# A float32 transformer on one core: the opening reordered, small transfers on GpSimd's queue

## The chip, the cores and the metric

One of the eight cores of a Trainium2 chip runs the kernel. A core has five engines with an instruction stream each: TensorE (PE in the profile, with its weight loads as PEld), VectorE (DVE), ScalarE (ACT), GpSimd (POOL) and SyncE (SP). Each runs its stream in order, and semaphores tie the streams together. Transfers are issued from an engine's queue (SP's, ACT's or POOL's) and are carried out by the core's 16 DMA engines. The metric is the device time of one execution in microseconds (us), the median over several.

## The reference

Input x is [1, 256, 1024], all in float32. Two layers of a block with five branches come first, then a block of gated linear attention with a feed-forward part, modulated by a vector c. Cut to what concerns the opening of the program:

```python
for l in range(2):
    h = rms_norm(x, norm_g[l])
    z = h @ w_in[l]                       # [256, IN_WIDTH], cut into 17 parts
    ...                                   # dsa, mla, diff, sgu branches on parts of z
    kv = rms_norm(mem, mem_norm_g) @ mem_w_kv[l]   # mem is [256, 1024]
    ...                                   # memory branch: attention of a part of z over kv
    x = x + (gates(z) * branches @ w_branch[l]) @ w_out[l]
...                                       # second block: GLA + MoBA, feed-forward 1024 -> 4096 -> 1024,
                                          # both scaled and shifted by silu(c) @ w_ada + b_ada
```

## The kernel before

The products are to have more than half of float32's digits, so each operand is split into a rounded part and a rest: for weights ACT writes `wh` (line 381) and DVE the rest `wl` (line 382), for activations ACT writes `hi` (line 579) and DVE `lo` (line 580). A weight matrix comes in pieces of 512 rows by 512 columns, held as four K tiles of 128 rows ([128, 4, 512], 1 MB). For each piece `mm_tok` runs 12 products for each of the two row tiles of 128 tokens: `wh·hi` and `wl·hi` for the four K tiles in turn (lines 431 and 432), then four `wh·lo` (line 434). 24 such products are a piece.

`run_stream` feeds the pieces through: `load(i)` issues piece i on SP's queue, AHEAD pieces early; `split(i)` makes `wh` and `wl`, LOOK pieces early, into LOOK + 1 = 4 pairs of buffers. Pieces 0 and 1 are two column groups (dv and du, which the sgu branch uses) times the first 512 rows, pieces 2 and 3 the same columns times the other 512 rows; pieces 4 and 5 are aq, 6 and 7 are 452 columns from ak on, and after one piece of `w_ada`, which DVE alone uses (lines 1330 and 1332), come the pieces of `mem_w_kv`. Piece 0 is loaded K tile by K tile.

The x operand is made in halves of 512 columns: `first_x(c)` transposes eight 128x128 blocks on PE (line 576 in `to_operand_g`) and splits them with the gain `norm_g` as a column (`gcol`); `gains_t(0)` has transposed that gain on PE (line 214) into `gT`. `gains_t(1)` does so for the other small vectors, which POOL's queue fetches in `first_loads`. Half 1 of x, `first_x(1)`, stands between pieces 0 and 1.

Work beside the pieces is written as generators in three lanes. `half(k)` is called after each row tile of a piece: it counts down what was deferred with `defer(fn, halves)` and steps lane 0 after the first row tile (k = 0), lanes 1 and 2 after the second. `angles` (rope tables) and behind it `mem_pre` stand in lane 1. `mem_pre` loads the two tiles of mem (line 739), takes four sums of squares on ACT (line 629), adds them up (line 747), makes the reciprocal root on DVE, scales the tiles there (line 750) and transposes them in 16 blocks for `mem_w_kv` (line 576).

A scheduler decides at build time how all this is interleaved: it fixes the order of each engine's stream from dependences and its own estimates, save where `pin` holds instructions at their place. The chip keeps that order. The lines of `evac_scaled` (729) scale and copy a finished sum from PSUM by the row factor `s`.

Of the kernel before, what the change touches and what calls it, by code (L numbers as in the profile page):

```python
# [57 lines left out]
def block_kernel(ctx: ExitStack, tc: tile.TileContext, a, out):  # L58
# [109 lines left out]
    def load_x(c):  # L168
        for t in range(2):
            SY.dma_start(x[t][:, c * 512:c * 512 + 512], xin[tsl(t), c * 512:c * 512 + 512])  # L170
# [5 lines left out]
    SY.dma_start(gains[0][:16, :], as_rows(a["norm_g"], 16))  # L176
    load_x(0)
# [14 lines left out]
    for _ in range(8):  # L192
        T.matmul(warm, ones, ones, start=True, stop=True)
# [48 lines left out]
    def angles():  # L242
        pf = small(8)
# [5 lines left out]
        yield  # L249
# [103 lines left out]
    def run_stream():  # L353
# [3 lines left out]
        def load(i):  # L357
# [3 lines left out]
            if i == 0:  # L361
                for k in range(nk):
                    SY.dma_start(v[:, k, :], bass.AP(tensor=src.tensor, offset=src.offset + k * src.ap[1][0],
                                                     ap=[src.ap[0], src.ap[2]]))
            else:
                SY.dma_start(v, src)
# [23 lines left out]

        load(0)
        load_x(1)
        load(1)
# [12 lines left out]
        pinned.extend(pieces[1:LOOK])  # L406
        for i in range(1, LOOK):
            split(i)
        for i in range(N):
            if i == 1:  # L410
                first_x(1, None)
# [4 lines left out]
            if i + LOOK < N and not late:  # L416
                split(i + LOOK)
# [6 lines left out]
            if i + LOOK < N and late:  # L424
                split(i + LOOK)

    def mm_tok(ps, xo, k0, hi, lo, nk, n, first, last, t):
# [5 lines left out]
        for i in range(nk):  # L433
            T.matmul(ps[:, :n], xo.lo[:, k0 + i, tsl(t)], hi[:, i, :n], start=False,  # L434
                     stop=last and i == nk - 1)

# [65 lines left out]
    def chunk_pair(ap, ops, cols, evacs, pres=None, post=None, rows=(0, 512), by_tile=False):  # L502
# [10 lines left out]
        for j in range(2):  # L513
            for q, (c0, n) in enumerate(cols):
                def fn(hi, lo, j=j, q=q):
                    if j == 0:
                        st[q] = [mbank(), mbank()]
                    if j == 0 or not by_tile:
# [50 lines left out]
    def to_operand_g(srcs, xo, n, g, step=None):  # L569

        for i0 in range(0, n, 2):
# [5 lines left out]
            for i in ks:  # L577
# [4 lines left out]
                if step:  # L582
                    step(i)

# [193 lines left out]
    def layer(l, h):  # L778
# [18 lines left out]
        def sgu():  # L797
            wr = slot([128, 8, 128])
            SY.dma_start(wr, a["sgu_w"][l].rearrange("g i j -> i g j"))
            lng, lnb = work([128, 512], "ln"), work([128, 512], "ln")  # L800
            SY.dma_start(lng, bc_row(a["sgu_ln_g"][l], 512))
            SY.dma_start(lnb, bc_row(a["sgu_ln_b"][l], 512))
# [152 lines left out]
        def diff_prep():  # L955
            lt = work([128, 256], "lam", bufs=1)
            SY.dma_start(lt, bc_row(a["diff_lambda"][l], 256))
            dg = wrk.tile([128, 128], F32, tag="dg", name=nm("dg"), bufs=1)
            SY.dma_start(dg, bc_row(a["diff_norm_g"][l], 128))
# [4 lines left out]
            V.tensor_scalar(dg, dg, 1.0 - LAM[l], None, op0=OP.mult)  # L964
# [810 lines left out]
```

## Time and profile before

| | |
|---|---|
| median of 3 runs | 1231.11 us (1230.07 to 1232.33) |
| the profiled execution | 1232.42 us, of it 1230.5 us span |
| PE busy | 1211.6 us, 98% of the span |
| DVE busy, ACT busy | 903.7 us (73%), 664.5 us (54%) |
| POOL busy | 14.8 us (1%) |
| DMA | 231.30 MB, mean 188 GB/s |

The span runs from the first to the last instruction that the profiler saw; the execution is 1.92 us longer. The granted clock of PE is given as a share of full speed (2.4 GHz), so 0.50 is 1.2 GHz.

### The profile page before, as it was taken

To read this page: it belongs to the slowest core of one execution; us is meant where nothing else is said; L and a number is where in the kernel's file an instruction comes from. 1 tells how busy PE (TensorE), PEld (TensorE's weight loads), DVE (VectorE), ACT (ScalarE), POOL (GpSimd) and SP (SyncE) were. 2 spreads that over 40 slices of the span, in tenths; PEclk is the share of its full clock that TensorE was granted. 3 is DMA by queue.
4 is the path that set the end of the run, shared out by engine and by line. 5 is a ranking of instruction groups with operands and counts; after the bars stand their busy time and mean duration, and the time that the engine had idled before them with its cause. 6 is when DMAs were issued, how large, how long until landed. Compare 5 with 4: busy or idle time off the path is not lost.

```text
span 1230.5 us, 17201 instructions
## 1 busy us (share of the span) xinstructions
PE 1211.6 (98%) x6497; PEld 1044.2 (85%) x6497; DVE 903.7 (73%) x1887; ACT 664.5 (54%) x1161; POOL 14.8 (1%) x35
## 2 busy tenths in 40 slices
PE   9999999999999999999999999999999999999997
PEld 7799888898888888898888988888878877899995
DVE  6866778768896777776887788876685877757665
ACT  6744645567465455546444756555455655545442
POOL 3000000000000000000000000000000000000000
PEclk9999999999999999999999999999988999999999
DMA  8855465544566465755565535656357724757650
GB/s 303 306 181 199 137 206 189 178 153 156 163 220 205 138 206 186 250 172 171 171 211 192 172 124 189 206 172 218 109 171 265 255 85 163 223 188 243 233 174 35
DMA packets 121284, 231.30 MB, mean 188 GB/s; under 512 B 5421, under 2 KB 17009, under 8 KB 121073
## 3 DMA queue, kind: packets, MB, share of 16 engines
q1 hardware_dynamic: 120880, 230.12, 56.8%
q8 instruction: 51, 0.84, 0.3%
q14 instruction: 33, 0.26, 0.1%
q0 software_dynamic: 320, 0.08, 0.1%
HBM read 229.10 MB, written 2.63 MB: 188 GB/s over the span
## 4 chain that ended last, share of the span: by engine, by line
PE 91%; DVE 4%; ACT 1%; DMA 1%; issue 1%; SPq 0%; ACTq 0%
PE pm L431 22%; PE pm L432 22%; PE pm L434 22%; PE pm L446 3%; PE pm L444 3%; PE pm L447 3%; PE po L703 3%; PE pm L552 3%; DVE wl L382 2%; PE pm L683 2%; DMA wt<-in_w_in_dram 1%; PE pm L1100 1%; PE pm L988 1%; PE pm L851 1%; PE po L434 1%
## 5 line engine op out<-in xcount | busy, mean ns | idle before, releaser
L382 DVE TENSOR_TENSOR wl<-wt,wh 128x1024 fp32r<-128x1024 f32 (+3 forms) x386 | 443.3, 1175 | 174.2 <-ACT wh L381 173.6
L381 ACT ACTIVATE wh<-wt 128x1024 fp32r<-128x1024 f32 (+3 forms) x386 | 379.5, 1019 | 272.1 <-PE pm L434 168.0
L431 PE MATMUL pm<-wh,hi 128*128 128x512 f32 (+4 forms) x1320 | 521.0, 396 | 4.0 <-ACT hi L598 2.6
L432 PE MATMUL pm<-wl,hi 128*128 128x512 f32 (+4 forms) x1320 | 509.5, 387 | 0.0
L434 PE MATMUL pm<-wh,lo 128*128 128x512 f32 (+4 forms) x1320 | 348.0, 384 | 0.0
L431 PEld LDWEIGHTS pm<-wh,hi 128*128 128x128 f32 x1320 | 251.3, 190 | 52.6 <-ACT hi L598 4.7
L432 PEld LDWEIGHTS pm<-wl,hi 128*128 128x128 f32 x1320 | 251.3, 190 | 45.6 <-DVE wl L382 0.6
L434 PEld LDWEIGHTS pm<-wh,lo 128*128 128x128 f32 x1320 | 246.5, 189 | 47.5
L446 PE MATMUL pm<-lo,wh 128*128 128x256 f32 x352 | 99.8, 284 | 2.9 <-DVE lo L580 2.9
L444 PE MATMUL pm<-hi,wh 128*128 128x256 f32 x352 | 100.6, 286 | 0.0
L447 PE MATMUL pm<-hi,wl 128*128 128x256 f32 x352 | 99.6, 284 | 0.0
L656 ACT ACTIVATE w<-w,s 128x256 f32<-128x256 f32 (+1 forms) x112 | 49.9, 446 | 39.0 <-DVE s L653 39.0
L446 PEld LDWEIGHTS pm<-lo,wh 128*128 128x128 f32 x352 | 67.8, 193 | 3.6 <-DVE lo L580 3.1
L444 PEld LDWEIGHTS pm<-hi,wh 128*128 128x128 f32 x352 | 67.9, 193 | 0.3
L447 PEld LDWEIGHTS pm<-hi,wl 128*128 128x128 f32 x352 | 67.7, 192 | 0.1
L1332 DVE SCALAR_TENSOR_TENSOR w<-wt,cact,w 128x512 f32<-128x512 f32 x84 | 62.7, 747 | 1.7 <-DMA wt<-in_w_ada_dram 0.6
L1146 ACT ACTIVATE t<-pm,s 128x512 f32<-128x512 f32 x40 | 27.5, 688 | 43.6 <-PE pm L434 43.6
L703 PEld LDWEIGHTS po<-t,w 128*128 128x128 f32 x352 | 46.0, 191 | 2.9
L552 PE MATMUL pm<-ident,t 128*128 128x128 f32 (+1 forms) x332 | 43.8, 273 | 1.6 <-DVE t L1282 1.6
L703 PE MATMUL po<-t,w 128*128 128x64 f32 (+1 forms) x352 | 44.8, 270 | 0.0
L552 PEld LDWEIGHTS pm<-ident,t 128*128 128x128 f32 (+1 forms) x332 | 38.4, 137 | 7.4 <-issue 2.4
L629 ACT ACTIVATE j<-t 128x512 f32<-128x512 f32 (+3 forms) x60 | 28.8, 479 | 28.1 <-DVE t L1682 14.1
(282 smaller groups left out, 1005.1 us busy)
## 6 DMA issues: line engine op xcount, KB each, us to landing
wt<-in_w_in_dram SPq DMA_DIRECT2D x99, 1024.0 KB, 5.0
wt<-in_w_ff_dram SPq DMA_DIRECT2D x32, 1024.0 KB, 5.4
wt<-in_w_ada_dram SPq DMA_DIRECT2D x24, 1024.0 KB, 5.2
wt<-in_w_branch_dram SPq DMA_DIRECT2D x20, 1024.0 KB, 5.1
wt<-in_w_out_dram SPq DMA_DIRECT2D x12, 1024.0 KB, 5.1
wt<-in_mem_w_kv_dram SPq DMA_DIRECT2D x8, 1024.0 KB, 7.3
wt<-in_w_in_dram SPq DMA_DIRECT2D x4, 904.0 KB, 5.5
wt<-in_w_in_dram SPq DMA_DIRECT2D x4, 768.0 KB, 4.4
```

The source lines that it names most:

```text
L381: pin(A.activation(hv[:, ks], wv[:, ks], AF.Copy), on)
L382: pin(V.tensor_tensor(lv[:, ks], wv[:, ks], hv[:, ks].bitcast(F32), OP.subtract), on)
L431: T.matmul(ps[:, :n], xh, hi[:, i, :n], start=first and i == 0, stop=False)
L432: T.matmul(ps[:, :n], xh, lo[:, i, :n], start=False, stop=False)
L434: T.matmul(ps[:, :n], xo.lo[:, k0 + i, tsl(t)], hi[:, i, :n], start=False, stop=last and i == nk - 1)
L444: T.matmul(ps, wh, xh, start=first and i == 0 and c % 2 == 0, stop=False, skip_group_check=True)
L446: T.matmul(ps, wh, xl, start=False, stop=False, skip_group_check=True)
L447: T.matmul(ps, wl, xh, start=False, stop=last and i == nk - 1, skip_group_check=True)
L552: T.transpose(ps[:, i, :], src[:, i * w:(i + 1) * w], ident)
L656: A.activation(p[:, k, :], p[:, k, :], AF.Exp, bias=mx[:, k:k + 1], scale=-1.0, accum_out=sm[:, k:k + 1])
L703: T.matmul(opsum[t][:, h, :], pt[:, k * nb + b, :], u["v"](h, b), start=b == 0, stop=b == nb - 1)
L1332: V.scalar_tensor_tensor(acc, w[:, i, :], B["c"][:, k:k + 1], acc, op0=OP.mult, op1=OP.add)
```

## The change

Of x, half 0 is fetched in four transfers of 256 columns instead of two of 512. `norm_g` and the first two K tiles of piece 0 are issued on ACT's queue, and a small activation behind them makes ACT load its function table there. Piece 1 is issued before half 1 of x. Two more warming products stand behind the first four transposes of x. Piece 0 is computed K tile by K tile for both row tiles (`mm_by_k`). The second half of x is deferred by three halves, so that it stands between the row tiles of piece 1, and the splits ahead are issued by `split_to`. `angles` goes to lane 0, with more steps, which leaves `mem_pre` first in lane 1. Some twenty small transfers (rows of gains and biases, `sgu_w`, the parameters of the second block) go from SP's queue to POOL's. In `diff_attn` one scaling of `dg` is folded into another instruction.

```diff
-    def load_x(c):
-        for t in range(2):
-            SY.dma_start(x[t][:, c * 512:c * 512 + 512], xin[tsl(t), c * 512:c * 512 + 512])
+    def load_x(c, n=512):
+        for c0 in range(c * 512, c * 512 + 512, n):
+            for t in range(2):
+                SY.dma_start(x[t][:, c0:c0 + n], xin[tsl(t), c0:c0 + n])
...
-    SY.dma_start(gains[0][:16, :], as_rows(a["norm_g"], 16))
-    load_x(0)
+    A.dma_start(gains[0][:16, :], as_rows(a["norm_g"], 16))
+    load_x(0, 256)
...
-    for _ in range(8):
-        T.matmul(warm, ones, ones, start=True, stop=True)
+
+    def warming(n):
+        for _ in range(n):
+            pin(T.matmul(warm, ones, ones, start=True, stop=True))
+
+    warming(8)
...
     def angles():
+        yield
...
-        yield
+        for _ in range(3):
+            yield
...
                 for k in range(nk):
-                    SY.dma_start(v[:, k, :], bass.AP(tensor=src.tensor, offset=src.offset + k * src.ap[1][0],
-                                                     ap=[src.ap[0], src.ap[2]]))
+                    q = A if k < 2 else SY
+                    q.dma_start(v[:, k, :], bass.AP(tensor=src.tensor, offset=src.offset + k * src.ap[1][0],
+                                                    ap=[src.ap[0], src.ap[2]]))
+                A.activation(first_act, ones[:, 0:1], AF.Copy)
...
         load(0)
+        load(1)
         load_x(1)
-        load(1)
         first_loads()
...
-        pinned.extend(pieces[1:LOOK])
-        for i in range(1, LOOK):
-            split(i)
+        pinned.extend(pieces[1:LOOK + 1])
+        split(1)
+        ahead = [2]
+
+        def split_to(i):
+            while ahead[0] <= min(i, N - 1):
+                split(ahead[0])
+                ahead[0] += 1
+
+        def second_x():
+            first_x(1, lambda i: None)
+            split_to(LOOK)
+
+        defer(second_x, 3)
         for i in range(N):
-            if i == 1:
-                first_x(1, None)
...
-            if i + LOOK < N and not late:
-                split(i + LOOK)
+            if i > 1 and not late:
+                split_to(i + LOOK)
...
+    def mm_by_k(ps, xo, hi, lo):
+
+        for i in range(4):
+            for t in range(2):
+                xh, xl = xo.hi[:, i, tsl(t)], xo.lo[:, i, tsl(t)]
+                T.matmul(ps[t], xh, hi[:, i, :], start=i == 0, stop=False)
+                T.matmul(ps[t], xl, hi[:, i, :], start=False, stop=False)
+                T.matmul(ps[t], xh, lo[:, i, :], start=False, stop=False)
...
+                    if by_k and j == 0 and q == 0:
+                        mm_by_k(st[q], ops[j](), hi, lo)
+                        half(0)
+                        half(1)
+                        return
...
+            if step and i0 == 0 and xo is E["x"][0]:
+                warming(2)
...
-            SY.dma_start(wr, a["sgu_w"][l].rearrange("g i j -> i g j"))
+            G.dma_start(wr, a["sgu_w"][l].rearrange("g i j -> i g j"))
             lng, lnb = work([128, 512], "ln"), work([128, 512], "ln")
-            SY.dma_start(lng, bc_row(a["sgu_ln_g"][l], 512))
-            SY.dma_start(lnb, bc_row(a["sgu_ln_b"][l], 512))
+            G.dma_start(lng, bc_row(a["sgu_ln_g"][l], 512))
+            G.dma_start(lnb, bc_row(a["sgu_ln_b"][l], 512))
...
-            V.tensor_scalar(dg, dg, 1.0 - LAM[l], None, op0=OP.mult)
...
-                V.tensor_tensor(ov, ov, dg[:, None, :].to_broadcast([128, 4, 128]), OP.mult)
+                V.scalar_tensor_tensor(ov, ov, 1.0 - LAM[l], dg[:, None, :].to_broadcast([128, 4, 128]), op0=OP.mult,
+                                       op1=OP.mult)
...
-            SY.dma_start(B["bias"][p], bass.AP(tensor=d.tensor, offset=d.offset + 384 * p + 127,
+            G.dma_start(B["bias"][p], bass.AP(tensor=d.tensor, offset=d.offset + 384 * p + 127,
...
-    lanes[1].add(angles())
+    lanes[0].add(angles())
     lanes[1].add(mem_pre())
```

Three places of the built programs show what moved. Names end in buffer numbers, which differ between the two programs; line 576 of before is line 609 after, 431 is 450, 432 is 451, 434 is 453, 382 is 391, and 750 is 785.

PE's stream where the blocks of mem (`t_424` and `t_425` before) are transposed; `pm_506` is the second row tile of piece 7. Before:

```order
L431 MATMUL pm_506<-wh_429,hi_133 128x452
L432 MATMUL pm_506<-wl_430,hi_133 128x452
L434 MATMUL pm_506<-wh_429,lo_134 128x452 x4
L576 MATMUL pm_598<-ident,t_424 128x128
L576 MATMUL pm_598<-ident,t_425 128x128
```

After, where `pm_448` is the second row tile of piece 5 and `pm_579` the first product of piece 6 (452 columns):

```order
L450 MATMUL pm_448<-wh_331,hi_135 128x512
L451 MATMUL pm_448<-wl_332,hi_135 128x512
L453 MATMUL pm_448<-wh_331,lo_136 128x512 x4
L609 MATMUL pm_489<-ident,t_234 128x128
L609 MATMUL pm_498<-ident,t_234 128x128
L609 MATMUL pm_553<-ident,t_234 128x128
L609 MATMUL pm_562<-ident,t_234 128x128
L450 MATMUL pm_579<-wh_376,hi_133 128x452
L609 MATMUL pm_489<-ident,t_235 128x128
```

The transposes of mem have moved ahead by the pieces 6 and 7, save for one product.

DVE's stream from the sum of mem's squares (`TENSOR_REDUCE`) on. Before; the scaling of the first tile of mem (line 750) stands 25 rows behind the first of these:

```order
L747 TENSOR_REDUCE s_539<-s_426 128x2
L238 TENSOR_SCALAR s_541<-s_539 128x2
L225 TENSOR_SCALAR s_544<-s_541 128x2
L226 TENSOR_SCALAR s_543<-s_541 128x2
L231 TENSOR_TENSOR s_545<-s_543 128x2
L808 BN_AGGR s_656<-st_657 128x2 x2
L232 TENSOR_TENSOR s_545<-s_545,s_544 128x2
L810 TENSOR_SCALAR s_662<-s_656 128x2
L233 SCALAR_TENSOR_TENSOR s_543<-s_545,s_543 128x2
L225 TENSOR_SCALAR s_665<-s_662 128x2
```

After, where the scaling (line 785) stands 29 rows behind the first:

```order
L782 TENSOR_REDUCE s_419<-s_236 128x2
L276 SCALAR_TENSOR_TENSOR w_467<-w_466,w_467 128x96
L243 TENSOR_SCALAR s_421<-s_419 128x2
L1368 SCALAR_TENSOR_TENSOR w_507<-wt_337,cact,w_507 128x512
L230 TENSOR_SCALAR s_424<-s_421 128x2
L231 TENSOR_SCALAR s_423<-s_421 128x2
L1368 SCALAR_TENSOR_TENSOR w_507<-wt_337,cact,w_507 128x512
L236 TENSOR_TENSOR s_425<-s_423 128x2
L276 SCALAR_TENSOR_TENSOR w_467<-w_465,w_467 128x96
L237 TENSOR_TENSOR s_425<-s_425,s_424 128x2
L391 TENSOR_TENSOR wl_572<-wt_382,wh_571 128x1024
```

The rest of the work on `w_ada` (line 1368, which was line 1332), rope steps (line 276) and the split of the first piece of `mem_w_kv` (`wl_572`) now stand between the sum and the scaling. Before, the split of the first piece of `mem_w_kv` and all of line 1332 stood ahead of the sum, and the split of the second piece (`wl_560`) between it and the scaling.

DVE's stream between the second half of x (`lo_136`) and the split of piece 2 (`wl_274`). Before, the copy to `gT` (line 215) stood further on, behind the split of piece 5. After:

```order
L613 SCALAR_TENSOR_TENSOR lo_136<-pm_264,gT,hi_135 128x256
L220 COPY gT<-pm_368 128x106
L271 TENSOR_SCALAR w_465<-w_465 128x96
L272 TENSOR_TENSOR w_466<-w_464,w_465 128x96
L391 TENSOR_TENSOR wl_274<-wt_158,wh_273 128x1024 x2
```

The copy, line 220 after, now stands ahead of the split of piece 2. On SP's queue the two loads of mem stood behind the first piece of `mem_w_kv` before and now stand between the loads of pieces 2 and 3; on POOL's queue `dg`, the two `sgu_ln` rows and `sgu_w` follow directly on the small vectors of `first_loads`.

## Rows read from the trace of the kernel before

**Rows 1.** The page, part 1: busy time, share and instructions of each engine.

```profile
PE 1211.6 (98%) x6497; PEld 1044.2 (85%) x6497; DVE 903.7 (73%) x1887; ACT 664.5 (54%) x1161; POOL 14.8 (1%) x35
```

**Rows 2.** Waits of PE: line, releaser, us in total, times, longest us.

```profile
PE pm L446 <- DVE lo L580: 2.9, 1, 2.9
...
PE pm L431 <- ACT wh L381: 1.3, 1, 1.3
```

**Rows 3.** Windows: us, busy of PE PEld DVE ACT POOL, PEclk, DMA share, GB/s.

```profile
0.00:5.00 5.00, 3.88 (x18) 3.73 (x18) 0.42 (x3) 0.00 (x0) 4.26 (x13) 1.00 0.47 134
5.00:10.00 5.00, 3.56 (x14) 2.43 (x15) 3.04 (x7) 4.47 (x8) 4.94 (x11) 0.79 0.97 332
10.00:15.00 5.00, 5.00 (x21) 3.86 (x21) 1.75 (x5) 2.03 (x4) 1.04 (x2) 0.86 1.06 370
27.50:53.80 26.30, 26.30 (x123) 22.62 (x122) 22.14 (x73) 20.22 (x31) 0.00 (x0) 1.00 0.83 289
59.20:62.50 3.30, 3.30 (x14) 2.91 (x13) 3.30 (x7) 2.40 (x5) 0.00 (x0) 0.50 0.74 264
14.80:53.20 38.40, 38.28 (x176) 31.92 (x176) 33.79 (x89) 31.43 (x51) 0.00 (x0) 1.00 0.89 309
```

**Rows 4.** Timeline of the opening: start, us, engine line op, count, idle before.

```profile
5.24 1.28 ACT L579 ACT_TABLE_LOAD   x1 [5.24 <-DVE gT L215]
...
7.62 0.98 PE L431 MATMUL pm<-wh,hi 128*128 128x512 f32 x2 [1.31 <-ACT wh L381]
...
13.68 2.01 ACT L381 ACTIVATE wh<-wt 128x1024 fp32r<-128x1024 f32 x2 [2.97 <-DMA wt<-in_w_in_dram]
...
14.77 2.36 DVE L382 TENSOR_TENSOR wl<-wt,wh 128x1024 fp32r<-128x1024 f32 x2 [3.02 <-ACT wh L381]
```

**Rows 5.** Timeline, DMA issues on SP and the transpose of the small vectors.

```profile
1.27 0.88 SPq L170 DMA_DIRECT2D t<-in_x_dram  x2
...
27.55 0.26 PE L214 MATMUL pm<-ident,w 106*128 106x106 f32 x1
...
33.64 0.97 SPq L739 DMA_DIRECT2D t<-in_mem_dram  x2
```

**Rows 6.** Timeline on the way to the operand of mem and behind it.

```profile
33.83 1.26 ACT L729 ACTIVATE t<-pm,s 128x512 f32<-128x512 f32 x2 [3.33 <-DVE s L233]
...
46.46 0.16 DVE L747 TENSOR_REDUCE s<-s 128x2 f32<-128x4 f32 x1 [0.63 <-ACT j L629]
...
51.82 1.42 DVE L750 TENSOR_SCALAR t<-t,s 128x1024 f32<-128x1024 f32 x2
...
53.78 1.91 PE L576 MATMUL pm<-ident,t 128*128 128x128 f32 x16
...
57.00 1.29 DVE L817 TENSOR_TENSOR t<-t,w 128x512 f32<-128x512 f32 x2
...
58.74 0.39 PE L446 MATMUL pm<-lo,wh 128*128 128x256 f32 x1 [2.93 <-DVE lo L580]
```

**Rows 7.** Lines by form, 14 to 56 us: count, busy, mean ns of one.

```profile
L382 DVE TENSOR_TENSOR wl<-wt,wh 128x1024 fp32r<-128x1024 f32 x16 | 19.0, 1220 | 4.0 <-ACT wh L381 4.0
...
L629 ACT ACTIVATE j<-t 128x512 f32<-128x512 f32 x8 | 5.0, 623 | 0.1
...
L381 ACT ACTIVATE wh<-wt 128x904 fp32r<-128x904 f32 x4 | 3.6, 956 | 0.4 <-DMA wt<-in_w_in_dram 0.4
...
L1332 DVE SCALAR_TENSOR_TENSOR w<-wt,cact,w 128x512 f32<-128x512 f32 x3 | 2.2, 750 | 0.1
...
L629 ACT ACTIVATION_READ_ACCUMULATOR j<-t 128x1 f32 x8 | 1.5, 190 | 0.0
```

**Rows 8.** A transfer on POOL's queue: KB, us from issue to landing.

```profile
invf<-in_invf_dram POOLq DMA_DIRECT2D x1, 24.0 KB, 6.3
```

**Rows 9.** Timeline of POOL and DVE around the bias of the second block.

```profile
929.85 0.63 POOL L1383 TENSOR_SCALAR_AFFINE_SELECT t<-t 128x512 f32<-128x512 f32 x1 [0.84 <-DMA t<-biasrows]
...
962.45 0.41 DVE L653 CUSTOM_DVE_ANT_0 w<-pm,t 128x256 f32<-128x256 f32 x1
```

More of the change, by code (lines that the diff above doesn't have):

```diff
@@ L389, in split @@
                     part(k, 2, pieces[i] in pinned)
+        first_act = small(1)
         load(0)
+        load(1)
         load_x(1)
-        load(1)
         first_loads()
@@ L423, in run_stream @@
                 fn(*P.pop(i))
-            if i + LOOK < N and late:
-                split(i + LOOK)
+            if late:
+                split_to(i + LOOK)
     def mm_tok(ps, xo, k0, hi, lo, nk, n, first, last, t):
@@ L500, in chunk_by_tile, with chunk_pair @@
         piece(wsrc(ap, 512, 4, c0, n), 4, n, f1, late=True)
-    def chunk_pair(ap, ops, cols, evacs, pres=None, post=None, rows=(0, 512), by_tile=False):
+    def chunk_pair(ap, ops, cols, evacs, pres=None, post=None, rows=(0, 512), by_tile=False, by_k=False):
         st = {}
@@ L956, in diff_prep @@
             lt = work([128, 256], "lam", bufs=1)
-            SY.dma_start(lt, bc_row(a["diff_lambda"][l], 256))
+            G.dma_start(lt, bc_row(a["diff_lambda"][l], 256))
             dg = wrk.tile([128, 128], F32, tag="dg", name=nm("dg"), bufs=1)
-            SY.dma_start(dg, bc_row(a["diff_norm_g"][l], 128))
+            G.dma_start(dg, bc_row(a["diff_norm_g"][l], 128))
             cq, ck = L["cq"], L["ck"]
@@ L1171, in mixT @@
                     B["fg"] = slot([128, D])
-                    SY.dma_start(B["fg"], bc_row(a["final_norm_g"], D))
+                    G.dma_start(B["fg"], bc_row(a["final_norm_g"], D))
                 L["mT"] = [Operand(), Operand()]
@@ L1193, in layer @@
         first = len(pieces)
-        chunk_pair(w_in, ops, [p_dv, p_du], [e_dv, e_du], pres={(1, 0): entry}, post=lambda: lanes[1].add(sgu()))
+        chunk_pair(w_in, ops, [p_dv, p_du], [e_dv, e_du], pres={(1, 0): entry}, post=lambda: lanes[1].add(sgu()),
+                   by_k=l == 0)
         p_aq, e_aq = tok("aq", COL["aq"], 512)
@@ L1350, in fin @@
                     V.tensor_copy(row, ps[0:1, :])
-                    SY.dma_start(adaR[q // 6][4 * (q % 6):4 * (q % 6) + 4, :], row)
+                    G.dma_start(adaR[q // 6][4 * (q % 6):4 * (q % 6) + 4, :], row)
                 else:
@@ L1356, in fin @@
                     br = B[name][:, c * 512:(c + 1) * 512]
-                    SY.dma_start(br, bc_row(a["b_ada_2"][0, q * 512:(q + 1) * 512], 512))
+                    G.dma_start(br, bc_row(a["b_ada_2"][0, q * 512:(q + 1) * 512], 512))
                     V.tensor_tensor(br, ps, br, OP.add)
@@ L1365, in bias_prep @@
         oh, rb = work([32, 384]), work([32, 8])
-        SY.dma_start(oh, a["onehot"])
-        SY.dma_start(rb, a["rel_bias_2"])
+        G.dma_start(oh, a["onehot"])
+        G.dma_start(rb, a["rel_bias_2"])
         ps = bbank([8, 384])
@@ L1372, in bias_prep @@
         dr = drm.tile([8, 384], F32, name="biasrow")
-        SY.dma_start(dr, sb)
+        G.dma_start(dr, sb)
         d, r2 = dr[0:1, :], drm.tile([128, 8 * 384], F32, name="biasrows")
-        SY.dma_start(r2, bass.AP(tensor=d.tensor, offset=d.offset, ap=[[0, 128], [1, 8 * 384]]))
+        G.dma_start(r2, bass.AP(tensor=d.tensor, offset=d.offset, ap=[[0, 128], [1, 8 * 384]]))
         B["bias"] = [slot([128, 4, 256]), slot([128, 4, 256])]
@@ L1423, in gla @@
         bg = work([128, 256])
-        SY.dma_start(wg, a["w_gla_gate_2"][0])
-        SY.dma_start(bg, bc_row(a["b_gla_gate_2"][0], 256))
+        G.dma_start(wg, a["w_gla_gate_2"][0])
+        G.dma_start(bg, bc_row(a["b_gla_gate_2"][0], 256))
         gm = work([128, 4, 128])
@@ L1533, in gla @@
         gob = work([128, 512])
-        SY.dma_start(gob, bc_row(a["g_gla_out_2"][0], 512))
+        G.dma_start(gob, bc_row(a["g_gla_out_2"][0], 512))
         V.tensor_scalar(gob, gob, 0.5, None, op0=OP.mult)
@@ L1660, in fn @@
                         B["gf"] = slot([128, D])
-                        SY.dma_start(B["gf"], bc_row(a["g_final_2"], D))
+                        G.dma_start(B["gf"], bc_row(a["g_final_2"], D))
                     if f == 7:
```

## The prediction

> **What bounds the kernel now.** I read the busy shares first, then the waits of PE, then windows of the opening, then the timeline around each wait. PE is busy 98% of the span [rows 1], so apart from the first microseconds the time is PE's work plus its few waits and its stretches at the lower clock. Two waits of PE lie where the change works: 1.3 us for the first `wh` and 2.9 us for `lo` of mem's operand [rows 2]. Between them PE waits for nothing: from 27.5 to 53.8 it is busy 26.30 of 26.30 us at a granted clock of 1.00 [rows 3]. Those 26.05 us (27.55 to some 53.6, without the last blocks) hold three pieces of 512 columns and two of 452 (0.883 of one), so a piece takes 26.05 / 4.766 = 5.47 us, a product 0.228 us. DVE has little air there: 33.79 of 38.40 us between 14.80 and 53.20 [rows 3]. So a change to the opening counts by what it does to PE's start, to DVE's order, and to the two waits.
>
> **The start.** Before, ACT's table load (1.28 us at 5.24) and then the first `hi` and `wh` stood ahead of the first product at 7.62 [rows 4]. The load leaves that path. What is late next is data: 134 GB/s for 5 us are 0.67 MB, then 332 GB/s [rows 3]. Both parts of x's half 0 and two K tiles of weights are 1.05 MB and share the engines, so they are through at 5 + 0.38/0.332 = 6.1. Piece 1, behind 3.15 MB, was through at 10 + 0.82/0.370 = 12.2 (0.67 + 1.66 = 2.33 MB by 10) and its first `wh` began at 13.68 [rows 3, 4], a lag of some 1.4. So x is there at 6.1 + 1.0 to 1.4, and the first product comes at 7.5 instead of 7.62; 6.3 (7.62 less 1.28) would be the best.
>
> SP takes 0.44 us for one issue [rows 5]; three issues leave it, 1.3 us of issue time at most, and the DMA share of 0.97 from 5 us on [rows 3] says that the engines, not the issuing, set the landings then. The Trainium skill ("DMA: Bandwidth & Descriptors", section "Issuing engines are not separate DMA queues") says that transfers begun by several engines run on the same 16 DMA engines and save only the time it takes to start them; by that rule the split over two queues is worth no more than that time, and the trace's share of 0.97 agrees.
>
> **Pieces 0 to 2.** Piece 0 by K tiles runs from 7.5 to some 13.0 (24 × 0.228). Piece 1 goes ahead of half 1 of x: 2.62 MB are through at 10 + 0.29/0.370 = 10.8, landed at 12.2. Its `wh` and `wl` take as long as before (13.68 to 17.13 [rows 4]), so `wl` is made from 13.4 to 15.8. So whatever the start gains before some 8 us, and what the lost stretch at a lower clock (0.79 over 5 to 10 [rows 3]) would give, is taken back by that wait. PE finishes row tile 0 of piece 1 at 17.4 and now makes eight transposes (1.1 us) there; `hi` and `lo` of half 1 follow while row tile 1 runs, and the small vectors are transposed at 21.3. DVE's copy of them and two rope steps stand ahead of `wl` of piece 2, so its first half is done at 23.4 while PE wants it at 21.95. Piece 2 ends at 28.4; before, the row behind it stood at 27.55 [rows 5]. The term is **+0.9**, between −0.9 (piece 1 lands 1 us sooner and `wl` of piece 2 is not late) and +1.3.
>
> **The operand of mem.** PE's rows now want the scaled tiles of mem after piece 5, at 28.4 + 3 × 5.47 = 44.8; before they were wanted after piece 7, at 53.78, and had been scaled from 51.82 to 53.24 [rows 6], hardly earlier. Is mem ready 8 us sooner? It is loaded sooner: its issue at 33.64 [rows 5] moves ahead of piece 3, to about 14. That takes 1.05 MB (and 1.1 MB more by POOL's queue) from pieces 3 and 4, which land at some 24.5 and 27.5. But loading was not its limit. ACT gets to the four sums of squares in its order behind the scaled copies, which wait for the root `s`: at 33.83 before [rows 6], at 35.4 after since the splits ahead of it on DVE come later. Then ACT does two copies (1.3), an activation (0.2), a `wh` (0.95), two copies (1.3), and four sums (0.62 + 0.19 each, less 0.06 of overlap) with two `wh` of 0.956 between them [rows 6, 7]: 35.4 + 1.3 + 0.2 + 0.95 + 1.3 + 3.0 + 1.9 = 44.05. The sum over them comes at 44.4 on DVE, where it was at 46.46.
>
> From that sum to the scaling took 51.82 − 46.46 = 5.36 us [rows 6], with two halves of a split (2 × 1.22 [rows 7]) and 23 small steps in it, so (5.36 − 2.44)/23 = 0.127 a step. After, DVE has there two halves of a split (2.44), two `w_ada` steps (1.5) [rows 7] and 25 small steps, seven of them for the rope tables (3.2): 7.1. The first tile is scaled at 51.5 + 0.7 = 52.2, the second at 52.9 (1.42 for both [rows 6]). PE waits from 44.8 to 52.2, less the little it can do between: **+7.0**.
>
> The bound from below: DVE's work up to the scaled tiles is 33.79 less one split of 2.44 [rows 3, 7], 31.4 us. It begins at 13.4 with `wl` of piece 1 and must idle between 15.8 and 18.5, since the `lo` of x's half 1 wait for row tile 0 of piece 1. 13.4 + 31.4 + 2.7 = 47.5, a wait of 2.7; rope steps can fill some of that idle time, so 2.0. From above: the sums 1 us later still, 8.5. I take 7.0, since ACT's and DVE's orders are fixed and the steps are counted in them.
>
> **What goes.** The wait of 2.93 at 58.74 [rows 6] falls away: `lo` of mem then stands ahead of the sgu steps of DVE, or is made while PE does pieces 6 and 7. After that wait PE ran at a clock of 0.50 from 59.2 to 62.5 [rows 3], 3.3 us for 1.65 us of work; a longer wait is followed by the like, so that stays, net 0. The transposes, products and splits are the same in number; two warming products lie in the wait for x, `by_k` reorders 24 products, the folded `dg` leaves one small DVE step out, all at nothing, under DMA's and PE's cover.
>
> **Small transfers on POOL's queue.** They take no time from an engine on the path: POOL is busy 14.8 us in all [rows 1]. A 24 KB transfer there took 6.3 us from issue to landing [rows 8]. The sgu rows are issued at about 14.5 and used first at 57.00 [rows 6]; the bias of the second block is ready at 930.5 and used at 962.45 [rows 9]: 32 us of cover. Cost 0; were a cover gone, the cost would be what the transfer is late.
>
> **Sum.** +0.9 + 7.0 − 2.9 = +5.0 on the profiled 1232.42 (1230.5 of span, 1.92 around it): 1237.4. That execution lies 1.31 above the median of the three runs, so **1236.1 us** against 1231.11.
>
> **The rivals.** Changes of 0.2%, 2.5 us, are about what can be told from none here: the bounds are 1228.6 and 1233.6.
>
> 1. Faster: mem is ready in time. Then the wait of 2.93 and its 1.65 at half clock go, and the start gives −0.9 to +0.9: 1231.1 − 4.6 ± 0.9, about **1226.5**. It decides at 44.8: the first tile must be scaled by then, 7.4 us sooner than in my chain, 2.7 sooner than the work bound allows, unless PE itself reaches that row later. For it speaks that mem lands some 20 us sooner; against it DVE's 33.79 of 38.40. Chance 0.18.
> 2. A wait as long as the old one: DVE and ACT close up, the wait for mem is 2.5 to 4.5. 1231.1 + 0.9 + 3.5 − 2.9 = **1232.6**. Chance 0.2.
> 3. POOL's transfers come late. As a mechanism here: DVE, busy 73% of the span [rows 1], holds up what POOL's queue issues, and a stage that lacks its row waits. The bias would have to be 32 us late [rows 9], the sgu rows 36. More than a wait of 1 or 2 us on top of the forecast (1238) I don't see. Chance 0.08. The Trainium skill ("SBUF — State Buffer", section "SBUF: two separate sides") warns of this: a transfer issued from GpSimd's queue can sit idle while certain DVE operations hold the port that its descriptors need. No row here shows such a delay; the 6.3 us of rows 8 is under light DVE load.
> 4. The change doesn't do what it says: the table load goes from the path and the first product still stands at 7.5. That is part of the forecast.
>
> **How the numbers follow.** The forecast (wait of 5 to 8.5, 1233.7 to 1238) has 0.54. Faster by over 0.2% is nearly all of rival 1: 0.17. Within: rival 2 less its edge, and what lies between it and rival 1: 0.21. Slower: 0.62. The likeliest case's own range is 1233.7 to 1238; for 8 in 10 the range takes in rival 2, half of rival 1 and the upper bounds (+1.3, 8.5): 1227.3 to 1239.3.
>
> **What would show it.** The first product at about 7.5; the table load at 1 to 3 us on ACT; piece 1's `wh` at 12.2; a wait of PE of about 1.4 before piece 2 for `wl`; in the list of waits line 609 for the scaled `t` of DVE with about 7 us, the scaling at about 51.5, and no wait of line 446's counterpart for `lo`. The prediction fails if the scaling stands at 46 or before, or if PE reaches the end of piece 5 after 47.

## The result, and the profile after

The changed kernel takes 1240.94 us (1238.95 to 1243.26, 4 runs) against 1231.67 us: ratio 1.0077, 95% interval 1.0062 to 1.0093. Slower was forecast, by 5.0 us; it is 9.3, and the median lies above the range's end of 1239.3. The profiled execution took 1243.26 us, 10.8 more than the profiled one of before.

The page's first part and the waits of PE (line, releaser, total us, times, longest) of the kernel after:

```profile
PE 1213.7 (98%) x6501; PEld 1044.9 (84%) x6501; DVE 905.3 (73%) x1885; ACT 665.8 (54%) x1162; POOL 33.9 (3%) x68
...
PE pm L609 <- DVE t L785: 6.4, 1, 6.4
PE pm L1481 <- ACT t L1610: 5.0, 1, 5.0
...
PE pm L451 <- DVE wl L391: 1.1, 2, 0.9
```

Of the two waits of [rows 2] neither is left, and two longer ones have come. The first is the wait for the scaled tiles of mem, forecast with 7.0 us. The second, of 5.0 us at line 1481, was not forecast. Windows of the kernel after, with the columns of [rows 3]:

```profile
0.00:5.00 5.00, 3.88 (x18) 3.73 (x19) 0.45 (x3) 1.49 (x2) 4.25 (x13) 1.00 0.56 161
5.00:10.00 5.00, 4.50 (x25) 3.63 (x25) 4.01 (x9) 3.87 (x8) 4.97 (x11) 1.00 1.04 375
...
48.80:55.70 6.90, 5.16 (x21) 4.89 (x22) 5.20 (x20) 5.94 (x11) 0.00 (x0) 0.51 0.66 243
922.60:932.90 10.30, 10.30 (x38) 9.24 (x38) 2.55 (x5) 0.05 (x1) 1.54 (x2) 0.50 0.96 315
939.70:946.50 6.80, 5.63 (x14) 4.01 (x14) 4.98 (x6) 2.62 (x7) 0.51 (x1) 0.50 0.76 258
```

The start is better: from 5 to 10 us it moves 375 GB/s in place of 332 [rows 3], and at full clock. Behind each of the two waits PE runs at 0.50, 1.2 GHz. The window of 922.6 to 932.9 is not of that kind: it stands ahead of the second wait, and PE is busy all through it. Before has the like:

```profile
919.20:929.40 10.20, 10.20 (x39) 9.14 (x39) 2.12 (x3) 3.05 (x6) 0.63 (x1) 0.50 0.97 309
```

The timeline of the opening of the kernel after, and then of the wait for mem:

```profile
2.21 1.28 ACT L373 ACT_TABLE_LOAD   x1 [2.21 <-issue]
...
7.07 0.47 PE L461 MATMUL pm<-wh,hi 128*128 128x512 f32 x1
...
10.80 2.01 ACT L390 ACTIVATE wh<-wt 128x1024 fp32r<-128x1024 f32 x2 [1.10 <-DMA wt<-in_w_in_dram]
...
25.14 2.01 ACT L390 ACTIVATE wh<-wt 128x1024 fp32r<-128x1024 f32 x2 [3.65 <-DMA wt<-in_w_in_dram]
...
43.81 0.15 DVE L782 TENSOR_REDUCE s<-s 128x2 f32<-128x4 f32 x1
...
49.74 1.41 DVE L785 TENSOR_SCALAR t<-t,s 128x1024 f32<-128x1024 f32 x2
...
50.54 1.12 PE L609 MATMUL pm<-ident,t 128*128 128x128 f32 x4 [6.42 <-DVE t L785]
```

First product 7.07 for 7.62, the load of the table off the path, piece 1 there at 10.80 for 13.68 [rows 4]. All that the start gained is gone by the end of piece 5, at 44.1 us (44.0 before), and mem is scaled at 49.74, 2.1 us sooner than before [rows 6], for a PE that wants it 9.7 sooner. The second wait, in the timeline of the kernel after (issues on POOL's and SP's queue, then ACT and PE):

```profile
919.42 0.55 POOL L1412 DMA_DIRECT2D biasrows<-biasrow  x1 [0.29 <-issue]
919.71 2.77 SPq L375 DMA_DIRECT2D wt<-in_w_in_dram  x2
...
932.85 2.01 ACT L390 ACTIVATE wh<-wt 128x1024 fp32r<-128x1024 f32 x2 [10.60 <-DMA wt<-in_w_in_dram]
...
938.71 1.06 ACT L390 ACTIVATE wh<-wt 128x1024 fp32r<-128x1024 f32 x1 [3.85 <-DMA wt<-in_w_in_dram]
939.67 1.22 ACT L1610 ACTIVATE t<-pm 128x512 f32<-128x512 f32 x4
...
940.87 0.38 PE L1481 MATMUL pm<-ident,t 128*16 128x128 f32 x1 [5.00 <-ACT t L1610]
```

And the same place before (SP's issues, then ACT; line 1574 became 1610):

```profile
914.25 0.58 SPq L1376 DMA_DIRECT2D biasrows<-biasrow  x1
916.34 0.39 SPq L366 DMA_DIRECT2D wt<-in_w_in_dram  x1
...
922.07 0.18 ACT L1574 ACTIVATE t<-pm 128x16 f32<-128x16 f32 x1 [2.18 <-PE pm L434]
924.63 0.18 ACT L1574 ACTIVATE t<-pm 128x16 f32<-128x16 f32 x1 [2.38 <-PE pm L434]
926.84 2.00 ACT L381 ACTIVATE wh<-wt 128x1024 fp32r<-128x1024 f32 x2 [2.03 <-DMA wt<-in_w_in_dram]
```

Two things differ. The two pieces of the columns mk, loaded beside the 1.5 MB that spread the rows of the bias, come later: the `wh` of the first begins 13.1 us after its issue, before 10.5. And ACT's stream has changed places: before, the copies of the gate's 16 columns out of PSUM (line 1574, `gg`) stand ahead of these pieces' `wh`; after, three halves of `wh` stand ahead of them. ACT sits in front of a late weight piece, and what PE waits for is queued behind it. The scheduler placed them so once the bias had left the weights' queue; the first experiments below show the order turning with the queue.

To compare executions, two products serve as marks that stand in all versions: A, the transposes at line 552 (585 after) behind a wait for DVE's `t`, and B, line 431 (450) behind ACT's `hi`. In the kernel after:

```profile
904.62 1.06 PE L585 MATMUL pm<-ident,t 128*128 128x128 f32 x8 [1.53 <-DVE t L1318]
...
1050.14 0.50 PE L450 MATMUL pm<-wh,hi 128*128 128x512 f32 x1 [1.17 <-ACT hi L633]
```

And before:

```profile
900.12 1.06 PE L552 MATMUL pm<-ident,t 128*128 128x128 f32 x8 [1.40 <-DVE t L1282]
...
1038.97 0.50 PE L431 MATMUL pm<-wh,hi 128*128 128x512 f32 x1 [1.17 <-ACT hi L598]
```

So 4.5 us are lost before A, 6.7 between A and B, and nothing behind B.

### The profile page after: what moved, and what is told of

The parts are those of the page before. It is cut to its first block, busy times and chain, and to the rows that moved or that the text cites. A ratio compares the mean times of both kernels' runs of the same rounds, so it can differ in the third digit from the quotient of the medians.

```text
span 1241.5 us, 17251 instructions
## 1 busy us (share of the span) xinstructions
PE 1213.7 (98%) x6501; PEld 1044.9 (84%) x6501; DVE 905.3 (73%) x1885; ACT 665.8 (54%) x1162; POOL 33.9 (3%) x68
## 4 chain that ended last, share of the span: by engine, by line
PE 89%; DVE 5%; DMA 3%; ACT 2%; issue 1%; SPq 0%; ACTq 0%
PE pm L450 22%; PE pm L451 22%; PE pm L453 21%; PE pm L475 3%; PE pm L474 3%; PE pm L472 3%; DMA wt<-in_w_in_dram 3%; PE po L738 3%; PE pm L585 3%; PE pm L718 2%; DVE wl L391 1%; PE pm L1135 1%; PE pm L1022 1%; ACT wh L390 1%; PE pm L886 1%
## 5 line engine op out<-in xcount | busy, mean ns | idle before, releaser
L450 PE MATMUL pm<-wh,hi 128*128 128x512 f32 (+3 forms) x1312 | 517.4, 395 | 2.9 <-ACT hi L633 2.5
L451 PE MATMUL pm<-wl,hi 128*128 128x512 f32 (+3 forms) x1312 | 506.3, 387 | 1.1 <-DVE wl L391 1.1
L453 PE MATMUL pm<-wh,lo 128*128 128x512 f32 (+3 forms) x1312 | 346.1, 385 | 0.0
```

The costliest lines, as they stand in the source:

```text
L450: T.matmul(ps[:, :n], xh, hi[:, i, :n], start=first and i == 0, stop=False)
L451: T.matmul(ps[:, :n], xh, lo[:, i, :n], start=False, stop=False)
```

## The experiments

| kernel | median us (runs) | ratio to before, interval | A | A to B | the same at full clock |
|---|---|---|---|---|---|
| before | 1231.67 (4) | | 900.12 | 138.85 | 132.1 |
| after | 1240.94 (4) | 1.0077, 1.0062 to 1.0093 | 904.62 | 145.52 | 137.6 |
| after_look | 1239.56 (1) | | 904.15 | 142.28 | 138.7 |
| a_bias_sp | 1231.23 (10) | 1.0006, 0.9993 to 1.0019 | 905.12 | 137.68 | 132.6 |
| a_bias_sp_2 | 1233.41 (1) | | 904.56 | 136.08 | 132.7 |
| b_bias_pool | 1234.92 (8) | 1.0030, 1.0018 to 1.0042 | 898.94 | 142.81 | 134.6 |
| a_bias_cut | 1239.22 (4) | 1.0065, 1.0049 to 1.0081 | 904.80 | 141.84 | 137.5 |
| a_evac_first | 1239.08 (5) | 1.0056, 1.0039 to 1.0073 | 905.21 | 139.56 | 133.0 |
| a_evac_first_look | 1238.26 (1) | | 905.22 | 139.92 | 134.8 |
| a_bias_early | 1233.93 (10) | 1.0018, 1.0009 to 1.0027 | 904.52 | 136.13 | 132.7 |
| a_mem_late | 1238.42 (4) | 1.0057, 1.0040 to 1.0074 | 903.25 | 142.23 | 137.2 |
| a_mem_late_bias_sp | 1231.94 (11) | 1.0008, 0.9999 to 1.0017 | 902.24 | 138.79 | 132.1 |
| b_mem_early | 1229.72 (10) | 0.9989, 0.9978 to 1.0000 | 901.62 | 134.41 | 132.7 |
| b_lo_first | 1226.99 (6) | 0.9956, 0.9939 to 0.9972 | 895.85 | 134.44 | 132.7 |
| a_mem_late_lo_first | 1229.47 (9) | 0.9979, 0.9969 to 0.9988 | 899.34 | 138.81 | 132.1 |
| a_small_sp | 1229.59 (10) | 0.9995, 0.9981 to 1.0009 | 901.63 | 134.43 | 132.7 |

The names with a_ start from the kernel after, those with b_ from the kernel before. Each ratio is to executions of before that were timed beside the kernel (their medians are 1231.36 to 1231.72). A and A to B are from the one traced execution of each. The last column takes off what half clock cost in that stage: for every half microsecond, PE's busy time times one less its clock. It is an estimate. Without a wait beyond the usual ones the stage takes 132.1 to 132.7 us in every kernel, and in the others it is longer by about their waits; so the rest of what A to B differs by is the clock.

**The bias on POOL's queue, undone and alone.** In `bias_prep`, five times (for b_bias_pool the other way round, on the kernel before):

```diff
-            G.dma_start(B["bias"][p], ...
+            SY.dma_start(B["bias"][p], ...
```

> The kernel after with the five transfers of bias_prep back on SP's queue. Theory P (the second loss of the kernel after, some 6.7 us of its profiled span, is the bias's broadcast on POOL's queue: it shares the DMA engines with two weight pieces, their wh come late, and the evacuations for which GLA's gate waits stand behind them on ACT): the wait of 5.0 us at line 1481 and the stretch at half clock behind it go, the span is about 1235 and the median about 1236. Rival (the wait is only the shifted schedule of the opening, whatever the queue): the wait stays at 4 to 5 us and the median at 1240 to 1241.

> The kernel before with only the five transfers of bias_prep on POOL's queue. Theory P: this part alone makes a wait of 3 to 5 us before the transposes of GLA's gate, and the median is 1235 to 1238. Rival: 1231 to 1232, no such wait.

Undone, the wait at line 1481 is gone and the median is before's: 9.7 us back, where some 5 were expected (1236). ACT's copies stand ahead of the late pieces' `wh` again (at 926.11 and 928.67, `wh` at 931.29). A second trace of it, a_bias_sp_2, has the same waits and less time at half clock; both traced executions (1235.60 and 1233.41 us) are slower than eight of its ten (1230.5 to 1231.6). Alone on top of the kernel before the edit costs 3.3 to 3.5 us, just under what was expected. The wait of 3 to 5 us before the gate's transposes didn't come (0.2); there is one of 2.0 us a little further on, in the same gate's chain:

```profile
PE pm L446 <- DVE lo L580: 3.2, 1, 3.2
...
PE pm L1472 <- DVE w L1457: 2.0, 1, 2.0
```

ACT's order has turned there too; its copies stand behind the first late piece, though not behind the second:

```profile
928.23 2.01 ACT L381 ACTIVATE wh<-wt 128x1024 fp32r<-128x1024 f32 x2 [9.15 <-DMA wt<-in_w_in_dram]
930.14 1.21 ACT L1574 ACTIVATE t<-pm 128x512 f32<-128x512 f32 x4
```

The rival, that the wait is only a consequence of the shifted opening, falls by both. That the same edit is worth 9.7 us on the one kernel and 3.4 on the other is in part the clock: at full clock the stage differs by 5.0 to 6.1 us in the one case and by 2.5 in the other.

**Smaller packets for the spread rows.**

```diff
-        G.dma_start(r2, bass.AP(tensor=d.tensor, offset=d.offset, ap=[[0, 128], [1, 8 * 384]]))
+        for e in range(8):
+            G.dma_start(r2[:, e * 384:(e + 1) * 384],
+                        bass.AP(tensor=d.tensor, offset=d.offset + e * 384, ap=[[0, 128], [1, 384]]))
```

> The kernel after with the 1.5 MB broadcast of the bias cut into eight transfers of 384 columns on the same queue (1536 byte packets in place of 12288); the order of instructions on PE, DVE and ACT is unchanged. If the weight pieces are late because the DMA engines take packets of the two queues in turn, and the large ones take most of the time: the first wh comes at about 927 in place of 932.85, the wait at line 1481 falls below 2 us, and the median is 1235 to 1238. If it is the sum of the bytes alone, or ACT's order alone: the wait stays at 4 to 5 us and the median at 1240 to 1241.

ACT's rows with the bias cut:

```profile
929.41 2.01 ACT L390 ACTIVATE wh<-wt 128x1024 fp32r<-128x1024 f32 x2 [6.99 <-DMA wt<-in_w_in_dram]
935.45 1.06 ACT L390 ACTIVATE wh<-wt 128x1024 fp32r<-128x1024 f32 x1 [4.03 <-DMA wt<-in_w_in_dram]
936.41 1.21 ACT L1612 ACTIVATE t<-pm 128x512 f32<-128x512 f32 x4
```

The first piece came 3.4 us sooner (929.41 for 932.85; 931.22 in the second trace of the kernel after), so large packets do push the weights aside: in the DMA records of the kernel after, from 921 to 927 us 115 packets of the bias (12288 bytes, 0.56 us each) passed beside 132 of the weights (2048 bytes, 0.15 us each), 1.41 MB beside 0.27 MB. With the cut it was 0.50 MB of the bias beside 1.07 MB of weights, though its packets were of 4608 and 3072 bytes there, not of 1536, and the eight issues took 4.2 us, so that a part of the gain may be the later start of these bytes. But the wait stayed at 4.8 us: the copies stand behind the second piece too, and that came at 935.45. Counted from A, the first piece was sooner than before (24.6 us for 26.7), and PE waited all the same. The packets' size is not the cause of the wait, only of a part of the lateness.

**ACT's order, with the bias still on POOL's queue.**

```diff
-                A.activation(B[name][:, t, :], ps, AF.Copy)
+                pin(A.activation(B[name][:, t, :], ps, AF.Copy), name in ("gqk", "gg"))
...
+        pinned.extend(pieces[first + 6:first + 8])
```

> The kernel after, the bias still on POOL's queue, with the four evacuations of gqk and gg held ahead of the splits of the mk pieces on ACT, as they stand in the kernel before. Theory O (the weight pieces are late behind the bias in every version; what costs the time is that ACT's stream has the splits of these late pieces ahead of the evacuations that PE waits for): the wait at line 1481 is under 1 us, the median 1231 to 1234. Theory P alone (late pieces cost the time by themselves): a wait of 3 to 5 us stands before a product of mq or mk instead, the median is 1238 to 1241.

> The kernel after with the evacuations first once more, since four of its five times (1237.9 to 1240.5) lie no lower than after's, though the profiled one has no wait at line 1481. Theory O: no wait over 1 us between 907 and 1040 us here either, and the excess is a longer opening or longer stretches at half clock. Rival (late pieces cost by themselves): this trace has a wait of 2 us or more for weights behind the bias.

ACT's rows with the copies ahead (first trace):

```profile
929.80 0.18 ACT L1610 ACTIVATE t<-pm 128x16 f32<-128x16 f32 x1 [2.38 <-PE pm L453]
933.48 2.01 ACT L390 ACTIVATE wh<-wt 128x1024 fp32r<-128x1024 f32 x2 [3.50 <-DMA wt<-in_w_in_dram]
```

The weight piece is as late as in the kernel after (933.48), and PE waits for nothing at line 1481 in either trace (the longest waits between A and B, the 1.2 at B apart, are 0.6 and 1.2 us). So the order turns the lateness into the wait. Yet the median came down by 1.9 us only, where 7 to 10 were expected. The two traces say in part why: with half clock taken off, the stage takes 133.0 and 134.8 us, against 137.6 and 138.7 in the kernel after and 132.1 to 132.7 without any such wait. The edit gives back nearly all that the stage had lost, and what half clock takes differs from trace to trace (8.0 and 3.6 us in the kernel after, 6.5 and 5.1 here). Theory O is shown for the wait and for the 5 to 6 us that go with it, not for the 9.7 us.

**The rows of the bias spread at the start of layer 1.** `bias_prep` is cut in two; the first part, up to the spread, is a lane of its own, begun behind layer 1's first pieces:

```diff
+                   post=lambda: (lanes[1].add(sgu()), l and lanes[2].add(bias_rows())),
```

> The kernel after with the first part of the bias (to the broadcast of 1.5 MB into DRAM) made at the start of layer 1, on POOL's queue as in after. The weight pieces of the second block then share the DMA engines only with the last 1 MB. Theory O and theory P both: the wait at line 1481 is under 1 us and the median 1230 to 1234. If POOL's queue is late for another reason (its issuing): the wait stays at 4 us or more.

1233.93 and no wait, with the transfer on POOL's queue all the same. ACT's order is that of before again (copies at 924.19 and 926.31, the late piece's `wh` behind them), so this edit takes away the lateness and the order together. POOL's queue as such is not late; it matters what the transfer runs beside. Issues on POOL took 0.5 us each (0.9 for `sgu_w`), and `sgu_w` there landed after 9.7 us in the opening where mem, on SP's queue, took 11.6. The delay of GpSimd's transfers by DVE, against which the Trainium skill warns ("SBUF — State Buffer", section "SBUF: two separate sides"), is not seen in these traces.

**Mem's place.** The transposes of mem moved back behind piece 7, without and with the bias on SP's queue; and the early place alone on top of the kernel before:

```diff
-        for _ in range(2):
+        for _ in range(5):
```

```diff
     def angles():
+        yield
...
-        yield
+        for _ in range(3):
+            yield
...
-    lanes[1].add(angles())
+    lanes[0].add(angles())
```

> The kernel after with three more steps of waiting in mem_pre ahead of the sums of squares, so that all 16 transposes of mem stand behind piece 7 again. Theory E (the first 4.35 us of the loss are the wait for mem's scaled tiles, 6.4 us in place of 2.9 for lo, and a longer stretch at half clock): the wait at line 609 on the scaled tiles is under 1 us, the loss by 903 us is between -1 and +1.5 us, the median 1236 to 1238. Rival (the splits of the opening as a whole are late, wherever mem stands): a wait of 4 us or more appears elsewhere before 75 us, the median is 1240 to 1241.

> The kernel after with both edits: mem's operand behind piece 7 again, and the bias back on SP's queue. If the two losses add up: the 2.5 us between the medians of after and of the kernel with mem late come off 1231.2, so 1228 to 1229.5, faster than before by 0.2%. If the opening gains nothing in itself: 1231 to 1232.

> The kernel before with one part of the change: angles in lane 0 with the yields of after, so that mem is loaded ahead of piece 3 and its transposes stand behind piece 5; the start, SP's other loads and the bias are as before. Theory E (the early place of mem costs by itself): a wait of 5 to 7 us for the scaled tiles, none for lo, the stage at 898.7 us comes 2 to 4 us later, the median 1233 to 1236. Rival (the wait is due to the new start): a wait under 3 us, the median 1230 to 1232.

With mem late the wait for the scaled tiles is 0.3 us, but the one for `lo` is back with 3.7, and A comes 1.4 us sooner only. With the bias on SP's queue as well the median is 1231.94: the two losses don't add up. The early place on top of the old start costs nothing; the median is 1.9 us below before's (interval 0.9978 to 1.0000). Its wait and its scaling, and then the wait, the sum and the scaling in the kernel with all small transfers on SP's queue (below):

```profile
PE pm L578 <- DVE t L752: 2.6, 1, 2.6
...
47.70 1.42 DVE L752 TENSOR_SCALAR t<-t,s 128x1024 f32<-128x1024 f32 x2
```

```profile
PE pm L609 <- DVE t L785: 3.5, 1, 3.5
...
42.08 0.15 DVE L782 TENSOR_REDUCE s<-s 128x2 f32<-128x4 f32 x1
...
48.07 1.41 DVE L785 TENSOR_SCALAR t<-t,s 128x1024 f32<-128x1024 f32 x2
```

Theory E falls in this form. Early, the wait replaces that for `lo` at about the same price; to 6.4 us it grows by something else. The sum over the squares stands at 43.88 here and at 43.81 in the kernel after; DVE's work from there to the scaling takes 3.8 and 5.9 us. Those 5.9 are DVE's order in the new program: with all small transfers on SP's queue they are 6.0 us too, but there the sum comes at 42.08, 1.7 us sooner. In the kernel after DVE had been held up by 2.95 us for the `wh` at 25.14, which waited 3.65 us for its piece; with the small transfers on SP's queue that `wh` waits for nothing.

**All small transfers on SP's queue, and the start alone.** The cause of the early loss was still open:

> The kernel after with all the small transfers back on SP's queue, not the bias alone. If only the bias counts: 1230.5 to 1232, as with the bias alone on SP (1231.23). If the others cost on POOL's queue too: 1228 to 1230. If they gain there: over 1232.

> The kernel after with mem's operand behind piece 7, the bias on SP's queue, and sgu's normalization behind mem's lo on DVE: what is left of the change is the start and the other small transfers on POOL's queue, on top of the faster DVE order. Against the kernel before with that DVE order alone (1226.99): if the new start gains, 1224 to 1226; if it is worth nothing, 1226 to 1228; if it costs by itself (piece 1 lands at 12 to 13 us in three of the traces, and DVE waits for the second half of x), 1228 to 1230.

With every small transfer back on SP's queue, the rest of the change is as fast as before (0.9981 to 1.0009), the wait for mem is 3.5 us in place of 6.4, and A is 3.0 us sooner than in the kernel after. Of the 2.9 us of the wait, 1.7 are mem's earlier scaling, and in the rest PE itself comes later. In the opening, POOL's queue carried 1.1 MB for sgu and diff at 13.5 to 16 us, beside mem and piece 3; on SP's queue only `dg` is issued there (16.3), the `sgu_ln` rows and `sgu_w` from 38 us on. The start by itself gives no gain: this kernel and the one with the early place alone (b_mem_early) differ by the start and the folded `dg`, and their medians (1229.59 and 1229.72), A (901.63 and 901.62) and A to B are the same. With the other DVE order it is 1229.47 on the new start, with the other small transfers on POOL's queue, and 1226.99 on the old one, though that order left a wait of 1.4 us for `lo` on the new start and 0.3 on the old.

**What the old wait was worth.** The kernel before, with sgu's normalization held behind mem's `lo` on DVE:

```diff
-                pin(V.scalar_tensor_tensor(xo.lo[:, i, :], pk, g(i), ...
+                marks["lo"] = pin(V.scalar_tensor_tensor(xo.lo[:, i, :], pk, g(i), ...
...
+                with behind("lo", l == 0):
                     V.tensor_scalar(dv[:, t, :], dv[:, t, :], mv[:, 2 * t:2 * t + 1], rs[:, t:t + 1],
```

> The kernel before with one edit that the change doesn't have: on DVE the normalization of sgu in layer 0 is held behind the eight lo of mem's operand. It tells what the wait of 2.93 us and the stretch at half clock behind it are worth. If the wait is DVE's order alone: it falls to about 0.7 us and the median to 1227 to 1229.5. If the work only stands elsewhere in PE's way: a new wait for sgu's values behind it, the median 1230.5 to 1232.

Waits of PE, and 55 to 65 us, in that kernel:

```profile
PE pm L446 <- DVE lo L580: 0.3, 1, 0.3
...
55.00:65.00 10.00, 9.67 (x74) 9.16 (x73) 9.20 (x18) 6.04 (x11) 0.00 (x0) 1.00 0.94 316
```

The wait is 0.3 us and the clock stays at 1.00 (the same ten microseconds before: PE busy 7.07, clock 0.83). 1226.99 us, 0.44% under before, is the best of all versions, and it needs none of the change. The half clock behind such a wait doesn't always come: in b_bias_pool the same wait is 3.2 us, and the same ten microseconds are at 1.00 throughout:

```profile
55.00:65.00 10.00, 6.78 (x50) 6.27 (x49) 9.96 (x19) 4.82 (x10) 0.00 (x0) 1.00 0.88 292
```

**A second trace of the kernel after.**

> The kernel after unchanged, for a second trace, since its times differ by 4 us (1238.95 to 1243.26). Both traces should show the wait for mem of 6 to 6.5 us and the wait at line 1481; theory O has the latter between 3 and 5 us, by how late the second mk piece lands, and the rest of the difference in the length of the stretches at half clock.

It has both waits, 5.5 and 5.8 us; both miss the expected ranges (6 to 6.5, 3 to 5), the first below and the second above.

## Why the prediction was right and wrong

**The direction.** Slower was forecast and came, but not by the parts that it was laid to. The +5.0 stood for the opening alone; with the whole change except the bias on POOL's queue the median is 1231.23 (0.9993 to 1.0019). By medians the steps from before to after are −1.9 for the early place of mem, −0.1 for the start, +1.6 for the other small transfers on POOL's queue and +9.7 for the bias there; the first three are hardly more than the intervals. That the direction was right is luck. Nor do the 4.5 us that the traces show at mark A, near the forecast 5.0, stand in the median of a_bias_sp, whose traces have the same loss there.

**The start** (+0.9, −0.9 to +1.3): first product 7.07 for a forecast 7.5, piece 1's `wh` at 10.80 for 12.2 (12.37 in the second trace), the wait for `wl` of piece 2 0.9 us for 1.4. Piece 5 ends at 44.1 in the first trace and at 45.4 in the second (PE then waits 6.42 and 5.5 us, to 50.54 and 50.9), where 27.57 + 3 × 5.47 = 44.0 held before: +0.1 and +1.4. Right in kind: what the start gained was taken back by the second half of x and by piece 2.

**The wait for mem** (+7.0): 6.4 and 5.5 us. Its place, its releaser and the sum over the squares (43.81 for 44.4) came as worked out from ACT's and DVE's orders; the scaling came at 49.74 for 51.5, since DVE's work between the two took 5.9 us for a forecast 7.1. The cause was put too narrowly: I laid the whole wait to mem's early place, and 2.6 to 3.5 us of it is there without small transfers on POOL's queue, in kernels that are no slower than before. With these transfers there the scaling comes at 49.5 to 50.9 in eight traces, without them at 48.07, and so some 2 us of the wait hang on them: I had them delay pieces 3 and 4 in the working, and then charged them nothing in their own part.

**What goes** (−2.9): right, no wait for `lo` is left. The stretch at half clock is longer than before's, 48.8 to 55.7, which the term of 0 missed by about 0.9 us ((55.66 − 50.54)/2 = 2.6 for 1.7). That a wait is followed by such a stretch was taken for granted; in b_bias_pool 3.2 us of it were not.

In the first trace these together are 4.5 us at mark A (0.1 + 6.4 − 2.9 + 0.9), for a forecast 5.0.

**Small transfers on POOL's queue** (0): the step that failed. The bias alone costs 9.7 us by the medians there, with a wait of 5.0 and 5.8 us at line 1481 in the traces. I asked only whether each row would land before it is used, found 32 us of cover for the bias, and that is still so: it was never late for its own reader. What it is late for is its neighbours. The Trainium skill's rule ("DMA: Bandwidth & Descriptors", section "Issuing engines are not separate DMA queues") says that transfers begun by several engines interleave on the same 16 DMA engines; I weighed it against the split of the start and not against this part, where the packets of 921 to 927 us agree with it. And I read the orders of the opening only, not of the second block, where ACT's rows had moved. My rival 3 had the wrong thing coming late and was priced at 1 to 2 us.

**What stays open.** Of the 9.7 us by medians, the order on ACT gives back 1.9 and the early spread 7.0. At full clock the stage from A to B loses 5.0 to 6.1 us to the bias, about as much as the wait, and the order gives back all but 0.4 to 2.2 of it. The rest is time at half clock, and that is not in the traces alone. The mean granted clock is on record for every execution; its median is 0.9895 in the kernel after, 0.991 with ACT's order turned back and 0.994 with the bias on SP's queue. Length times clock, an estimate of the time at full clock, has the medians 1226.7, 1223.9 and 1222.1, and 1218.8 to 1219.9 before. By it the bias costs 4.6 us, of which the order gives back 2.8, and the opening 2 to 3 that the medians don't show. Why the kernel after spends more time at half clock isn't shown. The order on ACT with pieces that come in time was not tried; the cut bias comes nearest to it.

## What to carry to other kernels

A transfer that is moved to another queue leaves the order that it kept with the others: ask what it now runs beside, not only whether it arrives in time. The scheduler's orders move with it: on both kernels, where the bias was spread from POOL's queue beside these pieces, it put their splits ahead of copies that PE needed first, so compare the orders of every engine at each place where a moved transfer is large. And a wait of PE can cost twice, once as idle time and once by the clock behind it: in the kernel before, a wait brought from 2.9 to 0.3 us was worth 4.6 by the medians and 4.3 at mark A, 2.6 of idle time and 1.65 of half clock. Last, take the time at half clock off before a trace is read for what an edit did in a stage.

## What the runs showed of the hardware

Executions of one kernel differ by several microseconds (1238.95 to 1243.26 for after, 1223.76 to 1229.38 for b_lo_first), and the traces show where: PE at 0.50 for stretches that come and go. One of them stands at the same place in all sixteen traces, and no wait stands shortly ahead of it: a little behind the start of the gate's products, which are 16 columns wide, PE falls to 0.50 while it is busy without a gap. Its length differs between executions of one program. In the two traces of the kernel after (the products begin at 920.04 and 919.56) it is 10.3 us, the window of 922.6 to 932.9 above, and 3.4:

```profile
920.04 0.17 PE L450 MATMUL pm<-wh,hi 128*128 128x16 f32 x1
```

```profile
924.70:928.10 3.40, 3.40 (x11) 2.72 (x11) 0.00 (x0) 0.00 (x0) 0.16 (x1) 0.50 0.87 282
```

That these narrow products bring it about was not tried. From A to B the work is the same; without a wait beyond the usual ones it took 134.4 us in three kernels, whose window in a_small_sp has a clock of 0.99, and 138.9 in the kernel before, with 0.95:

```profile
901.60:1036.00 134.40, 131.61 (x693) 107.10 (x693) 104.13 (x261) 78.04 (x156) 6.45 (x10) 0.99 0.62 205
```

```profile
900.10:1039.00 138.90, 136.21 (x694) 111.31 (x694) 103.79 (x261) 78.03 (x156) 4.51 (x10) 0.95 0.60 199
```

So two traces can differ by 4.4 us in a stage that a change doesn't touch, and only medians of many executions, the waits, or a stage with its half clock taken off say what an edit did.
